# Turning the softmax results by VectorE's 32x32 transpose and a round trip through memory in place of TensorE's transposes

## The chip, the cores and the metric

One core of a Trainium2 chip runs the whole program. The metric is the device time of one execution in microseconds.

## What is computed

One layer of an encoder over two sequences of 512 tokens with 1024 channels, each with 256 memory tokens. After an RMS norm, one input projection gives the inputs of three branches (a state space model called S5, differential attention, cross-attention to the memory) and 3 x 1024 gates. The branches are projected up, gated and added, and an output projection and a feed-forward layer follow. The change concerns the two attentions. Cut to them:

```python
# cross-attention, 4 heads of 128, 256 memory tokens per sequence
s = jnp.einsum('blhd,bmhd->bhlm', q, mk).astype(jnp.float32) * (X_DH ** -0.5)
probs = jax.nn.softmax(s, axis=-1).astype(mv.dtype)
return jnp.einsum('bhlm,bmhd->blhd', probs, mv).reshape(Bn, L, X_WIDTH)

# differential attention, 4 heads with two maps of 64 each, 512 keys
s = jnp.einsum('bqhd,bkhd->bhqk', qblk, k).astype(jnp.float32) * scale
probs = jax.nn.softmax(s, axis=-1).reshape(Bn, DIFF_HEADS, 2, Q_BLOCK, L)
w = probs[:, :, 0] - lam * probs[:, :, 1]
return jnp.einsum('bhqk,bkhe->bqhe', w.astype(v.dtype), v)
```

## The kernel before

Every wide product is done in three passes of a rounded type: a value is split into a high part (a cast on ScalarE) and a low part (a subtraction on VectorE), and hi x hi, hi x lo and lo x hi are added in one PSUM bank. `split` issues that pair; `wf` is a weight as loaded (512 KB, two buffers), `wh` and `wl` are its parts.

The order of instructions on VectorE, ScalarE, GpSimd and SyncE is set by a scheduler. On TensorE it is the order of the program from the cross-attention on (`PE.on = True`). The kernel weaves two things there by hand: the steps of an attention, and *filler*, which is independent projection work. `units` is a generator for one 128-column tile of a projection: 48 products of 512 columns, handed out six at a time. `queue` is the list of such generators (queries of later heads, gates, values, then the branches' up projections, `merges`), and `fill(n)` issues about n of their products.

Cross-attention: 32 steps (4 heads, 2 sequences, 4 query tiles of 128). A step makes the scores of 128 queries against 256 memory tokens in a bank `sc`, and `softmax_parts` takes the maximum (`nb`, VectorE), the exponential `e` with its sum (ScalarE), and the reciprocal `r` (VectorE), after which VectorE scales `e`. The output product needs the keys on partitions, and so `e` is transposed: two transposes with `ident` on TensorE into a bank `tr` (`aux`), from where `split` takes them to `xpTh`, `xpTl`. After four steps the output product goes into a bank `oo`, and is stored to `bD`. Beside this, `Prepare` loads pieces of a later weight (`raw`), adds them on GpSimd, splits them (`hl`) and stores them (`wD`).

Differential attention: again 32 steps of 128 queries, now against 512 keys and with two maps. `score` makes both maps' exponentials and their weighted difference `e0`; `turn` transposes it with four TensorE transposes and splits it into `pH`, `pL`; `outputs` follows after every second step, `squares` and `normed` (the norm of a head's output, with transposes of their own in `tr`) after every fourth. The loop's lag is written out in its conditions, for example

```python
        if 0 < i <= n and steps[i - 1][2] % 2:
            outputs(i - 1)
```

In both stages the PSUM has eight banks: two `mm` (filler), three `sc`, two `tr`, one `oo`. All loads and stores of both stages are issued by SyncE, in one order.

Of the kernel before, what the change touches and what calls it, by code (L numbers as in the profile page):

```python
# [19 lines left out]
P = 128  # L20
L = 512
# [49 lines left out]
def encoder(ctx: ExitStack, tc: tile.TileContext, a, out, out_t):  # L71
# [68 lines left out]
    def split(hi, lo, src, scale=None):  # L140
# [6 lines left out]
            l_ = V.scalar_tensor_tensor(out=lo, in0=src, scalar=scale, in1=hi.bitcast(F32), op0=ALU.mult, op1=ALU.subtract)  # L147
        return h, l_

    last_w = last_s = None  # L150

    def weight_in(src, n=DM, parts=1, eng=SP):
# [138 lines left out]
    def mem_k(h, w):  # L291
        nonlocal mf
        o = aux()
        for i in range(KD):
            mm3([o], *w, [(mhk[i], mlk[i])], i, KD)
        if h % 2 == 0:
            mf = slot("ld", [P, 2, L], name="mf")
        S.copy(mf[:, h % 2], o)
        return mf

    ob = []
# [174 lines left out]
    for n in range(-(-(NC - 2) // STEPS)):  # L476
        wn = gate_w()
        next(s5)
        gate(*w)
        w = wn  # L480
        if n in (3, 4):
            ssm = sums(a["memN"], "ld", ss=None if n == 3 else ssm, ts=range(2 * n - 6, 2 * n - 4))
        if n == 5:
            rs_, bc = factor(ssm, DM)
            V.tensor_copy(mrs, rs_)
            S.copy(mbc, bc)
    for n in NG[1]:
        if n:
            wn = gate_w()
# [171 lines left out]
    queue = []  # L661
    owed = 0

    def fill(n):
        nonlocal owed
        owed += n
        while owed > 0 and queue:
            r = next(queue[0], None)
            if r is None:
                queue.pop(0)  # L670
            else:
                owed -= r
        if not queue:
            owed = 0
# [2 lines left out]
        while any(g is g_ for g_ in queue):  # L677
            fill(1)

    def units(src, hi, lo, use, nk=KD):  # L680

        wh, wl = weight(src, nk * P)
        for s in range(NS):
            cs = slice(s * L, (s + 1) * L)
            o = bank()
            for k in range(nk):
                mm3([o], wh, wl, [(hi[k][:, cs], lo[k][:, cs])], k, nk)
                if k == nk - 1:
                    use(s, o)
                if k % 2 == 1:  # L690
                    yield 6

    def gate_units():
        t = next(todo)
        gt = slot("ld", name="gt")

        def use(s, o):
            S.activation(out=gt[:, s * L : (s + 1) * L], in_=o, func=AF.Tanh, scale=0.5)

        yield from units(a["w_in"][20 + t], xh, xl, use)  # L700
        SP.dma_start(gD[t], gt)

    def v_units(hf, res):

        ws = [weight(a["w_v"][hf, c]) for c in range(2)]
        for s in range(NS):
            vh, vl = (slot("v2" if hf == 1 and s == 0 else "v", [P, 4, 256], F32R, n_) for n_ in ("vh", "vl"))
            for i2 in range(2):
                ob = bank()
                for kt in range(KD):  # L710
# [12 lines left out]
            res.append((vh, vl))  # L723
# [3 lines left out]
    def xq_units(h):  # L727
        def use(s, o):
            qs[h, s] = tuple(xa.tile([P, L], F32R, tag=n_, name=n_, bufs=3) for n_ in ("qh", "ql"))
            split(*qs[h, s], o)  # L730

        return units(a["w_in"][16 + h], xh, xl, use)

    ahead = [x_ for x_ in pieces if x_[2]]
    pes = ExitStack()
# [4 lines left out]
    for _ in xq_units(0):  # L740
        pass
    xq = {h: xq_units(h) for h in range(1, 4)}
    queue += [xq[1], gate_units(), xq[2], xq[3], v_units(0, v0), units(a["w_in"][4], xh, xl, dq0.__setitem__)]
    PE.on = True
    steps = [(h, s, lt) for h in range(4) for s in range(NS) for lt in range(4)]
    es, pT = {}, {}
    AHEAD = 2
    fill(6)
    for i in range(-AHEAD, len(steps) + 1):
# [19 lines left out]
        fill(4)  # L769
        if 0 <= i < len(steps):  # L770
            h, s, lt = steps[i]
            if lt == 0:
                pT[h, s] = tuple(slot("xT", [P, 2, L], F32R, n_) for n_ in ("xpTh", "xpTl"))
            e = es.pop(i)
            tr = aux()
            for j in range(2):
                PE.transpose(tr[:, j * P : (j + 1) * P], e[:, j * P : (j + 1) * P], ident)
            split(*(p_[:, :, lt * P : (lt + 1) * P] for p_ in pT[h, s]), tr[:, : 2 * P].rearrange("p (j q) -> p j q", j=2))
        fill(5 if i < len(steps) else 18)
        if i > 0 and steps[i - 1][2] == 3:  # L780
            h, s, _ = steps[i - 1]
            pTh, pTl = pT.pop((h, s))
            oo = bank("oo")
            hs = slice(h * P, (h + 1) * P)
# [24 lines left out]
    def rotated(is_q):  # L809
# [6 lines left out]
        def use(s, o):  # L816
# [8 lines left out]
            split(hl[:, 0], hl[:, 1], t1, scale=0.125 if is_q else None)  # L825
# [11 lines left out]
    qk = {}  # L837

    def qk_units(h, is_q):
        qk[h, is_q], use = rotated(is_q)  # L840
        yield from units(a["w_in"][(4 if is_q else 8) + h], xh, xl, use)


    mg = [None] * KD
# [10 lines left out]
        return list(zip(*(merge_part(n, t, tags[t]) for t in range(4))))  # L855

    def merge_units(n, b, m, first=False, last=False):
        gt = slot("ld", name="gl")
        SP.dma_start(gt, gD[n * KD + m])
        if first:  # L860
# [7 lines left out]
        yield from units(a["w_up"][n, m], *b, use, 4)  # L868
        if not first:
            PO.tensor_tensor(out=mg[m], in0=mg[m], in1=gt, op=ALU.add)  # L870
        if last:
# [10 lines left out]
            b0.append(list(zip(*(parts0[t_] for t_ in range(4)))))  # L882

    def merges():
        res_.close()
        xp_es.close()
        open_tags(mes, side="right", mg=8, y=8)
        for m in range(KD):
            if m == 5:
                b2 = merge_in(2)  # L890
            yield from merge_units(0, b0[0], m, first=True)
        for m in range(KD):
            yield from merge_units(2, b2, m)

    qk[0, True], use = rotated(True)
    for s in range(NS):
        use(s, dq0[s])
    for _ in qk_units(0, False):  # L900
        pass
    for _ in gate_units():
        pass
# [2 lines left out]
    queue += [qk_units(1, True), dk[1], gate_units(), qk_units(2, True), dk[2], v1_, qk_units(3, True), dk[3], gate_units(),  # L906
              gate_units(), merges()]
    s0, ss, osb = {}, {}, {}

    def score(i):  # L910
        nonlocal last_e
# [13 lines left out]
            er.append(softmax_parts(ap_, acol, sc[mp], L, 1.0, f"d{mp}", None if mp else s0[h, s][:, qt : qt + 1]))  # L925
        (e0, sm0), (e1, r1) = er
        V.scalar_tensor_tensor(out=r1, in0=r1, scalar=nlam, in1=sm0, op0=ALU.mult, op1=ALU.mult)
        last_e = last_x, V.scalar_tensor_tensor(out=e0, in0=e1, scalar=r1, in1=e0, op0=ALU.mult, op1=ALU.add)
        es[i] = e0

    def turn(i):
        h, s, qt = steps[i]
        if qt % 2 == 0:
            pT[h, s, qt // 2] = tuple(slot("pT", [P, 4, 2 * P], F32R, n_) for n_ in ("pH", "pL"))
        e0 = es.pop(i)
        tr = aux()
        for j in range(4):
            PE.transpose(tr[:, j * P : (j + 1) * P], e0[:, j * P : (j + 1) * P], ident)
        ps = slice(qt % 2 * P, qt % 2 * P + P)
        split(*(p_[:, :, ps] for p_ in pT[h, s, qt // 2]), tr.rearrange("p (j q) -> p j q", j=4))  # L940

    def outputs(i):

# [35 lines left out]
        SP.dma_start(bD[1, h, :, s * L : (s + 1) * L], osb[h, s])  # L979

    n = len(steps)
    for i in range(-1, n + 3):
        if i + 1 < n:
            score(i + 1)
        if i in (22, 23):
# [9 lines left out]
        if 1 < i <= n + 1 and steps[i - 2][2] == 3:  # L995
            squares(i - 2)
        if i > 2 and steps[i - 3][2] == 3:
            normed(i - 3)
    aes.close()
    phase.close()  # L1000
    ves.close()
# [16 lines left out]
        b1.append(merge_part(1, len(b1), "zzzy"[len(b1)]))  # L1018
    b1 = list(zip(*b1))
    for m in range(KD):  # L1020
        for _ in merge_units(1, b1, m, last=True):
            pass


# [1096 lines left out]
```

## Time and profile before

| | |
|---|---|
| median of 3 runs | 1583.21 us (1581.76 to 1584.73) |
| profiled execution: its time, its span | 1582.8 us, 1581.0 us |
| granted clock of TensorE | 0.999 |
| TensorE, VectorE, ScalarE, GpSimd busy | 1572.9, 1118.4, 628.3, 511.0 us |
| DMA | 261.06 MB, 165 GB/s over the span |

Busy time counts an instruction from its start to its end; matmuls overlap, so that what one of them costs is seen from start to start. A row of groups gives the line, engine, operation, out<-in, the count, the busy time, the mean duration of one, and the idle time before it with its releaser. Line 62 is a helper through which nearly all instructions are issued, so groups are read by the names of tiles. A DMA share is the mean busy share of the 16 DMA engines; the DMA view counts packets by size.

### The profile page before, as it was taken

What the parts mean: (1) busy time and instruction counts of PE and PEld (TensorE: products, weight loads), DVE (VectorE), ACT (ScalarE), POOL (GpSimd) and SP (SyncE); (2) the same over time, 40 slices, a digit from 0 to 9 for tenths busy, and PEclk for the clock granted to TensorE, in tenths of its full rate; (3) what the DMA queues carried; (4) which work ended last, traced back from release to release, by engine and by line L of the source; (5) the groups of instructions that cost most, each with busy time, mean ns of one, the idle gap of its engine ahead of it and who ended that gap; (6) DMA issues with size and microseconds to landing.
All of it is one profiled execution on the core that took longest, in us unless ns stands there. A gap on an engine that the chain in (4) does not pass through costs nothing.

```text
span 1581.0 us, 21523 instructions
## 1 busy us (share of the span) xinstructions
PE 1572.9 (99%) x7697; PEld 1321.3 (84%) x7697; DVE 1118.4 (71%) x1777; ACT 628.3 (40%) x1112; POOL 511.0 (32%) x406
## 2 busy tenths in 40 slices
PE   9999999999999999999999999999999999999998
PEld 8888888888898889888888888888888888788887
DVE  5797788565765776766445567777767777999664
ACT  7354333244543366564223353333333323333222
POOL 0001000001433221300343345767655542455352
PEclk9999999999999999999999999999999999999999
DMA  9543372556655543355544433555433241786632
GB/s 362 202 147 135 109 269 80 190 188 211 207 174 176 138 114 93 104 184 167 183 156 149 152 101 126 184 183 179 163 124 133 107 152 69 274 280 203 212 120 107
DMA packets 118971, 261.06 MB, mean 165 GB/s; under 512 B 15824, under 2 KB 51920, under 8 KB 118864
## 3 DMA queue, kind: packets, MB, share of 16 engines
q1 hardware_dynamic: 117424, 255.46, 48.6%
q10 hardware_dynamic: 1440, 4.22, 0.7%
q8 instruction: 61, 1.00, 0.3%
q14 instruction: 46, 0.38, 0.1%
HBM read 172.89 MB, written 74.15 MB: 156 GB/s over the span
## 4 chain that ended last, share of the span: by engine, by line
PE 94%; DMA 2%; DVE 2%; SPq 0%; issue 0%; ACT 0%; DVEq 0%; ACTq 0%
PE bkmm L62 82%; PE bktr L62 8%; PE bksc L62 3%; PE bkoo L62 2%; DMA zu<-uD 1%; SPq L62 0%; DMA yD<-y__2104 0%; DMA lv<-in_lamv 0%; DMA acc<-in_w_fo 0%; DMA zy<-yD 0%; DVE zu L62 0%; DVE y L62 0%; DMA wf<-in_w_mv 0%; DVE ts L62 0%; DVE zy L62 0%
## 5 line engine op out<-in xcount | busy, mean ns | idle before, releaser
L62 PE MATMUL bkmm<-xh,wh 128*128 128x512 f32 x640 | 252.7, 395 | 0.0
L62 PE MATMUL bkmm<-xl,wh 128*128 128x512 f32 x640 | 250.8, 392 | 0.0
L62 PE MATMUL bkmm<-xh,wl 128*128 128x512 f32 x640 | 250.0, 391 | 0.2 <-DVE wl L62 0.2
L62 PE MATMUL bkmm<-th,whl 128*128 128x512 f32 x696 | 227.2, 389 | 0.0
L62 ACT CAST wh<-wf 128x1024 fp32r<-128x1024 f32 (+1 forms) x131 | 116.1, 887 | 231.9 <-PE bkmm L62 199.5
L62 DVE TENSOR_TENSOR wl<-wf,wh 128x1024 fp32r<-128x1024 f32 (+1 forms) x132 | 140.6, 1065 | 65.4 <-ACT wh L62 62.4
L62 PEld LDWEIGHTS bkmm<-th,whl 128*128 128x128 f32 x696 | 130.6, 188 | 27.2 <-issue 0.2
L62 PEld LDWEIGHTS bkmm<-xh,wl 128*128 128x128 f32 x640 | 120.2, 188 | 26.1 <-DVE wl L62 0.7
L62 PE MATMUL bkmm<-th,w 128*128 128x512 f32 x432 | 140.4, 391 | 0.3
L62 PEld LDWEIGHTS bkmm<-xl,wh 128*128 128x128 f32 x640 | 120.4, 188 | 23.2 <-issue 0.6
L62 PEld LDWEIGHTS bkmm<-xh,wh 128*128 128x128 f32 x640 | 120.3, 188 | 23.2 <-issue 0.2
L62 POOL TENSOR_TENSOR raw<-raw 128x128 f32<-128x128 f32 x144 | 88.2, 613 | 156.7 <-DMA raw<-in_w_fo 107.1
L62 PE MATMUL bkmm<-tl,whl 128*128 128x512 f32 x348 | 135.4, 389 | 0.0
L62 POOL TENSOR_TENSOR ws<-wf 128x512 f32<-128x512 f32 x44 | 71.8, 1632 | 147.2 <-DMA wf<-in_w_fu 147.2
L62 DVE TENSOR_TENSOR whl<-ws,whl 128x1024 fp32r<-128x1024 f32 x44 | 77.2, 1755 | 57.5 <-ACT whl L62 57.5
L62 PE MATMUL bkmm<-th,wh 128*128 128x512 f32 x260 | 101.3, 390 | 0.0
L62 PE MATMUL bkmm<-th,wl 128*128 128x512 f32 x260 | 101.2, 389 | 0.0
L62 PE MATMUL bkmm<-tl,wh 128*128 128x512 f32 x260 | 101.2, 389 | 0.0
L62 PEld LDWEIGHTS bkmm<-th,w 128*128 128x128 f32 x432 | 80.9, 188 | 19.5 <-DVE nsq L62 1.1
L62 POOL TENSOR_TENSOR mg<-mg,gl 128x1024 f32<-128x1024 f32 x16 | 44.2, 2764 | 136.4 <-DMA bD<-osb 94.1
L62 PE MATMUL bkmm<-tl,w 128*128 128x512 f32 x216 | 84.1, 389 | 0.0
L62 ACT ACTIVATE e<-bksc,nb 128x512 f32<-128x512 f32 (+1 forms) x96 | 58.9, 616 | 60.8 <-DVE nb L62 60.1
(644 smaller groups left out, 3600.4 us busy)
## 6 DMA issues: line engine op xcount, KB each, us to landing
wf<-in_w_in SPq DMA_DIRECT2D x40, 512.0 KB, 4.4
wD<-hl SPq DMA_DIRECT2D x36, 512.0 KB, 2.9
w<-wD SPq DMA_DIRECT2D x36, 512.0 KB, 3.7
gD<-gt SPq DMA_DIRECT2D x24, 512.0 KB, 3.0
gl<-gD SPq DMA_DIRECT2D x24, 512.0 KB, 3.4
raw<-in_w_fo SPq DMA_DIRECT2D x88, 128.0 KB, 3.0
wf<-in_w_fg SPq DMA_DIRECT2D x22, 512.0 KB, 3.8
wf<-in_w_fu SPq DMA_DIRECT2D x22, 512.0 KB, 3.5
```

Source lines behind the costliest of these rows:

```text
L62: ins = do(*args, **kw)
```

## The change

No transpose of an attention's result is left on TensorE. In both attentions VectorE transposes the result `e` in blocks of 32x32 (`et`; in the differential attention into the buffer of the second map), SyncE stores it to memory (`xD`, `eD`), and `turned` loads it back with four loads, one for each 32 partitions, in which the blocks change places, into a tile `tn` of 128x1024 that is split as a whole. That is done once for four cross steps and once for two differential steps. So that a load reads runs of 32 columns times the number of key tiles (256 B with 256 memory tokens, 512 B with 512 keys), the keys' columns are permuted beforehand by `by_row` and `by_tile`, where the keys are written anyway. The scaling of `e` in the cross-attention moves from VectorE to ScalarE.

The output products move later: in the cross-attention from one step behind the block's last turning to six (the loop has 38 turns and `fill` gives 8 or 10 in each, 9 before), in the differential attention from one step to three, and `squares` and `normed` to four and six. A weight's load is now issued when its unit becomes the second in the queue, apart from the split (`yield 0` and `begun`). The value units take both banks of a sequence in turn, and the banks are three `mm`, three `sc`, one `tr`, one `oo`.

```diff
+    def turned(hl, src, nt):
+        nonlocal last_t
+        n = 32 * nt
+        t_ = slot("ld", [P, DM], name="tn")
+        tv = t_.rearrange("p (k f) -> p k f", f=n)
+        for d in range(4):
+            last_t = SP.dma_start(tv[32 * d : 32 * d + 32], src.rearrange("k (b x) f -> x (k b) f", b=4)[:, :, n * d : n * d + n])
+        split(*(p_.rearrange("p t (k q) -> p t k q", q=32) for p_ in hl), tv.rearrange("p k (t q) -> p t k q", q=32))
...
-    open_banks(mm=2, sc=3, tr=2, oo=1)
+    open_banks(mm=3, sc=3, tr=1, oo=1)
...
         while owed > 0 and queue:
+            for g in queue[:2]:
+                if not any(g is g_ for g_ in begun):
+                    begun.append(g)
+                    next(g)
...
-            last_e = last_x, V.tensor_scalar_mul(e, e, r)
-            es[i + AHEAD] = e
+            S.activation(out=e, in_=e, func=AF.Copy, scale=r)
+            et = xa.tile([P, NMEM], F32, tag="xt", name="et", bufs=4)
+            last_e = last_x, V.transpose(et, e)
+            SP.dma_start(xD[(i + AHEAD) // 4 % 2, lt], et)
...
-            if lt == 0:
+            if lt == 3:
                 pT[h, s] = tuple(slot("xT", [P, 2, L], F32R, n_) for n_ in ("xpTh", "xpTl"))
-            e = es.pop(i)
-            tr = aux()
-            for j in range(2):
-                PE.transpose(tr[:, j * P : (j + 1) * P], e[:, j * P : (j + 1) * P], ident)
-            split(*(p_[:, :, lt * P : (lt + 1) * P] for p_ in pT[h, s]), tr[:, : 2 * P].rearrange("p (j q) -> p j q", j=2))
-        fill(5 if i < len(steps) else 18)
-        if i > 0 and steps[i - 1][2] == 3:
+                turned(pT[h, s], xD[i // 4 % 2], 2)
+        fill(4 if i < 30 else 6)
+        if i >= 6 and steps[i - 6][2] == 3:
...
-        last_e = last_x, V.scalar_tensor_tensor(out=e0, in0=e1, scalar=r1, in1=e0, op0=ALU.mult, op1=ALU.add)
-        es[i] = e0
+        V.scalar_tensor_tensor(out=e0, in0=e1, scalar=r1, in1=e0, op0=ALU.mult, op1=ALU.add)
+        last_e = last_x, V.transpose(e1, e0)
+        SP.dma_start(eD[i // 2 % 4, i % 2], e1)
...
-        e0 = es.pop(i)
-        tr = aux()
-        for j in range(4):
-            PE.transpose(tr[:, j * P : (j + 1) * P], e0[:, j * P : (j + 1) * P], ident)
-        ps = slice(qt % 2 * P, qt % 2 * P + P)
-        split(*(p_[:, :, ps] for p_ in pT[h, s, qt // 2]), tr.rearrange("p (j q) -> p j q", j=4))
+            turned(pT[h, s, qt // 2], eD[i // 2 % 4], 4)
...
-        if 0 < i <= n and steps[i - 1][2] % 2:
-            outputs(i - 1)
+        if 3 <= i < n + 3 and steps[i - 3][2] % 2:
+            outputs(i - 3)
```

On TensorE, in the middle of the cross-attention, before (`bktr`, `bksc`, `bkoo`, `bkmm` are the banks, the products of `xh`, `xl` with `wh`, `wl` are filler):

```order
L62 MATMUL bkmm<-xh_132,wl 128x512
L62 MATMUL bktr<-ident,e 128x128 x2
L62 MATMUL bksc<-mkvh,qh 128x256
L62 MATMUL bksc<-mkvl,qh 128x256
L62 MATMUL bksc<-mkvh,ql 128x256
L62 MATMUL bkmm<-xh_133,wh 128x512
```

and now, where an output product stands right before a step's scores:

```order
L62 MATMUL bkmm<-xh_134,wl 128x512
L62 MATMUL bkoo<-xpTh,mkvh 128x512
L62 MATMUL bkoo<-xpTl,mkvh 128x512
L62 MATMUL bkoo<-xpTh,mkvl 128x512
L62 MATMUL bkoo<-xpTh,mkvh 128x512
L62 MATMUL bkoo<-xpTl,mkvh 128x512
L62 MATMUL bkoo<-xpTh,mkvl 128x512
L62 MATMUL bksc<-mkvh,qh 128x256
L62 MATMUL bksc<-mkvl,qh 128x256
L62 MATMUL bksc<-mkvh,ql 128x256
```

The pairs of transposes are gone from every step, and scores and output products alone are left between the filler.

On SyncE, in the same part of the program, before (`raw` and `wD` belong to `Prepare`):

```order
L62 DMA wD_2_3128<-hl 128x1024
L62 DMA raw<-in_w_fo 128x256
L62 DMA raw<-in_w_fo 128x2x128
L62 DMA gD<-gt 128x1024
L62 DMA wf<-in_w_v 128x1024
L62 DMA bD<-xosb 128x512
L62 DMA wD_0_3129<-hl 128x1024
```

and now:

```order
L62 DMA xD<-et 128x256 x2
L62 DMA wD_1_3132<-hl 128x1024
L62 DMA raw<-in_w_fo 128x256
L62 DMA raw<-in_w_fo 128x2x128
L62 DMA xD<-et 128x256 x2
L62 DMA wD_2_3133<-hl 128x1024
L62 DMA raw<-in_w_fo 128x256
L62 DMA tn<-xD 32x16x64 x4
L62 DMA raw<-in_w_fo 128x2x128
L62 DMA wf<-in_w_v 128x1024
```

Each block of four steps has put four stores and four loads between the transfers that stood there, and the loads wait for the stores.

More of the change, by code (lines that the diff above doesn't have):

```diff
@@ L297, in mem_k @@
             mf = slot("ld", [P, 2, L], name="mf")
-        S.copy(mf[:, h % 2], o)
+        for s in range(NS):
+            cs = slice(s * NMEM, (s + 1) * NMEM)
+            S.copy(by_row(mf[:, h % 2, cs], 2), by_tile(o[:, cs], 2))
         return mf
@@ L485, in encoder @@
             V.tensor_copy(mrs, rs_)
-            S.copy(mbc, bc)
+            for s in range(NS):
+                cs = slice(s * NMEM, (s + 1) * NMEM)
+                S.copy(by_row(mbc[:, cs], 2), by_tile(bc[:, cs], 2))
     for n in NG[1]:
@@ L824, in use @@
             hl = slot("ld", [P, 2, L], F32R, "hl")
-            split(hl[:, 0], hl[:, 1], t1, scale=0.125 if is_q else None)
+            if is_q:
+                split(hl[:, 0], hl[:, 1], t1, scale=0.125)
+            else:
+                split(*(by_row(hl[:, j], 4) for j in range(2)), by_tile(t1, 4))
             for mp in range(2):
@@ L839, in qk_units @@
     def qk_units(h, is_q):
+        u = units(a["w_in"][(4 if is_q else 8) + h], lambda s, o: use(s, o))
+        yield next(u)
         qk[h, is_q], use = rotated(is_q)
-        yield from units(a["w_in"][(4 if is_q else 8) + h], xh, xl, use)
+        yield from u
     mg = [None] * KD
@@ L857, in merge_units @@
     def merge_units(n, b, m, first=False, last=False):
+        u = units(a["w_up"][n, m], lambda s, o: use(s, o), 4, b)
+        yield next(u)
         gt = slot("ld", name="gl")
@@ L884, in merges @@
     def merges():
+        g = merge_units(0, lambda: b0[0], 0, first=True)
+        yield next(g)
         res_.close()
@@ L887, in merges @@
         open_tags(mes, side="right", mg=8, y=8)
[L888 to L893, printed above, removed]
+        b2 = []
+        for i in range(2 * KD):
+            if 2 <= i < 6:
+                b2.append(merge_part(2, i - 2, "y"))
+            if i + 1 < KD:
+                nxt = merge_units(0, lambda: b0[0], i + 1, first=True)
+            elif i + 1 < 2 * KD:
+                nxt = merge_units(2, lambda: list(zip(*b2)), i + 1 - KD)
+            if i + 1 < 2 * KD:
+                next(nxt)
+            yield from g
+            g = nxt
     qk[0, True], use = rotated(True)
@@ L899, in encoder @@
         use(s, dq0[s])
-    for _ in qk_units(0, False):
+    u = qk_units(0, False)
+    with tc.issue_after(last_t.ins):
+        next(u)
+    for _ in u:
         pass
@@ L981, in encoder @@
     n = len(steps)
-    for i in range(-1, n + 3):
+    for i in range(-1, n + 6):
         if i + 1 < n:
@@ L991, in encoder @@
             turn(i)
-        if 0 < i <= n and steps[i - 1][2] % 2:
-            outputs(i - 1)
+        if 3 <= i < n + 3 and steps[i - 3][2] % 2:
+            outputs(i - 3)
         fill(10)
[L995 to L998, printed above, removed]
+        if 4 <= i < n + 4 and steps[i - 4][2] == 3:
+            squares(i - 4)
+        if i >= 6 and steps[i - 6][2] == 3:
+            normed(i - 6)
     aes.close()
@@ L1020, in encoder @@
     for m in range(KD):
-        for _ in merge_units(1, b1, m, last=True):
+        for _ in merge_units(1, lambda: b1, m, last=True):
             pass
```

47 lines of the change are left out of this document (31 added, 16 removed).

## The prediction

> **What bounds the kernel now.** I read the page first, then TensorE's own waits, then the two attentions by windows, then single matmuls in the timeline, and last the groups of operations and the DMA view of the same windows. From the page (share of the span by engine, then the chain that ended last):
>
> ```profile
> span 1581.0 us, 21523 instructions
> PE 1572.9 (99%) x7697; PEld 1321.3 (84%) x7697; DVE 1118.4 (71%) x1777; ACT 628.3 (40%) x1112; POOL 511.0 (32%) x406
> PE 94%; DMA 2%; DVE 2%; SPq 0%; issue 0%; ACT 0%; DVEq 0%; ACTq 0%
> ```
>
> TensorE is busy for 99% of the span and carries 94% of the chain. Its waits on other engines (total us, times, longest) are four single ones over the whole span, and the longest is
>
> ```profile
> PE bkmm L62 <- DVE ident L62: 1.1, 1, 1.1
> ```
>
> So there is nothing on TensorE's side to be won but its own work. The windows are the cross-attention (first score to last output product), the differential attention, and one stretch that I need for the DMA engines:
>
> ```profile
> core 0: us, PE busy (x) PEld busy (x) DVE busy (x) ACT busy (x) POOL busy (x), PEclk, DMA share, GB/s
> 390.00:497.00 107.00, 107.00 (x638) 93.88 (x637) 72.92 (x202) 54.97 (x144) 38.50 (x66) 1.00 0.56 187
> 518.00:745.00 227.00, 227.00 (x1271) 195.90 (x1270) 166.06 (x311) 128.60 (x292) 37.09 (x24) 1.00 0.45 131
> 320.00:332.00 12.00, 12.00 (x54) 9.94 (x53) 7.10 (x22) 3.65 (x5) 0.00 (x0) 1.00 0.91 273
> ```
>
> In both attentions TensorE never stops, at full granted clock. What is taken off it is therefore saved, one for one, as long as what replaces it stays under cover; what replaces it lands on VectorE (68% and 73% busy) and on the DMA engines (0.56 and 0.45).
>
> **What is removed.** 192 transposes `bktr<-ident,e`, two in each of 32 cross steps and four in each of 32 differential steps:
>
> ```profile
> L62 PE MATMUL bktr<-ident,e x192: 270/272/276, 396.6 to 739.7; 128*128 128x128 f32 x192
> ```
>
> The bar of 272 ns is not the price, since matmuls overlap. The price is what a transpose adds between starts. One cross step and one differential step of TensorE's timeline (start, length):
>
> ```profile
> 484.47 0.39 PE L62 MATMUL bkmm<-xh,wl 128*128 128x512 f32 x1
> 484.71 0.38 PE L62 MATMUL bktr<-ident,e 128*128 128x128 f32 x2
> 484.84 0.48 PE L62 MATMUL bkmm<-xh,wh 128*128 128x512 f32 x1
> 485.16 0.39 PE L62 MATMUL bkmm<-xl,wh 128*128 128x512 f32 x1
> ...
> 621.71 0.28 PE L62 MATMUL bkmm<-wh,xl 128*128 128x256 f32 x1
> 621.83 0.60 PE L62 MATMUL bktr<-ident,e 128*128 128x128 f32 x4
> 622.18 0.36 PE L62 MATMUL bkoo<-pH,vh 128*128 128x256 f32 x1
> 622.38 0.28 PE L62 MATMUL bkoo<-pL,vh 128*128 128x256 f32 x1
> ```
>
> From 484.71 to 485.16 are 0.45 us for two transposes and a 512-wide product, which alone takes 0.23 (484.47 to 484.71 is 0.24): 0.22 us a step. From 621.83 to 622.38 are 0.55 us for four transposes and a 256-wide product of 0.12 (621.71 to 621.83): 0.43 us. 32 x 0.22 + 32 x 0.43 = 7.0 + 13.8 = **20.8 us**, all of it on the path. Since TensorE has no idle time here, this is also the most that the change can bring.
>
> **VectorE and ScalarE.** The groups of the two attentions (count | busy us, mean ns):
>
> ```profile
> L62 DVE TENSOR_REDUCE nb<-bksc 128x1 f32<-128x256 f32 x31 | 13.1, 421 | 10.3 <-PE bksc L62 9.6
> L62 DVE TENSOR_TENSOR xpTl<-bktr,xpTh 128x256 fp32r<-128x256 f32 x29 | 12.0, 413 | 0.1
> L62 DVE TENSOR_SCALAR e<-e,r 128x256 f32<-128x256 f32 x31 | 11.7, 376 | 0.7
> L62 DVE TENSOR_TENSOR wl<-wf,wh 128x1024 fp32r<-128x1024 f32 x7 | 9.0, 1281 | 6.1 <-ACT wh L62 6.1
> L62 ACT ACTIVATE e<-bksc,nb 128x256 f32<-128x256 f32 x31 | 14.8, 477 | 21.2 <-DVE nb L62 21.1
> L62 ACT CAST xpTh<-bktr 128x256 fp32r<-128x256 f32 x29 | 10.8, 373 | 6.4 <-PE bktr L62 6.2
> L62 ACT CAST wh<-wf 128x1024 fp32r<-128x1024 f32 x6 | 6.3, 1050 | 1.9 <-PE bkmm L62 1.9
> L62 DVE TENSOR_TENSOR pL<-bktr,pH 128x512 fp32r<-128x512 f32 x31 | 21.2, 683 | 1.5 <-ACT pH L62 1.3
> L62 DVE TENSOR_TENSOR wl<-wf,wh 128x1024 fp32r<-128x1024 f32 x10 | 14.2, 1422 | 0.0
> L62 DVE STREAM_SHUFFLE t<-bkmm 128x512 f32<-128x512 f32 x12 | 8.8, 736 | 0.0
> L62 ACT ACTIVATE acc<-bktr 128x128 f32<-128x128 f32 x28 | 7.4, 278 | 5.3 <-PE bktr L62 5.3
> ```
>
> No row shows the 32x32 transpose. Its nearest row is the shuffle, which also rearranges within 32 partitions: 736 ns for 512 columns. I take 0.74 us and 0.37 for 256 columns; the lower end is pL's 683, the upper twice the shuffle, 1.47, if filling and draining do not overlap. Cross: the scaling (32 x 0.376) goes to ScalarE, the subtractions from PSUM (32 x 0.413) become 8 on 1024 columns like wl (8 x 1.28): 72.9 - 12.0 - 13.2 + 11.8 + 10.2 = 69.7 us in the 100.0 that are left (107 - 7.0), 70%. Differential: 166.1 - 32 x 0.683 + 16 x 1.422 + 32 x 0.74 = 166.1 - 21.9 + 22.8 + 23.7 = 190.7 in 213.2 (227 - 13.8), 89%. I add **2 us** for this: the queue of VectorE is in order, and where a maximum comes late, the `sc` banks are held and the next scores wait; the ends are 0 and, at 1.47, the rival below. ScalarE stays about where it was: 32 scalings at some 0.37 come, and casts of 1024 columns at 1.05 take the place of four or two smaller ones.
>
> The Trainium skill (VectorE: DVE Perf Modes, The three transpose paths) has 311 ns for a 128x128 bf16 transpose on VectorE; by an estimate of four such, 1.24 us, the differential stage would hold 206.7 us of VectorE work, 97%, and the sum below would come to some 1586. No row here shows the operation.
>
> **The DMA engines.** New are 32 stores of 128 KB and 32 loads in runs of 256 B (cross), 32 stores of 256 KB and 64 loads in runs of 512 B (differential). The DMA view of the cross window, then of 80.5 to 85 us, where nearly all packets are 512 B, then of 48 to 49.2, where loads of 128 B a partition pass:
>
> ```profile
> DMA packets 10875, 20.06 MB, mean 187 GB/s; under 512 B 1008, under 2 KB 6384, under 8 KB 10864
> q1 hardware_dynamic: 10864, 19.93, 55.4%
> wf<-in_w_in SPq DMA_DIRECT2D x5, 512.0 KB, 3.7
> bD<-xosb SPq DMA_DIRECT2D x7, 256.0 KB, 2.4
> ...
> DMA packets 1083, 0.54 MB, mean 119 GB/s; under 512 B 122, under 2 KB 1073, under 8 KB 1081
> q1 hardware_dynamic: 1081, 0.52, 40.8%
> ...
> DMA packets 317, 0.21 MB, mean 178 GB/s; under 512 B 231, under 2 KB 231, under 8 KB 317
> q1 hardware_dynamic: 317, 0.21, 81.8%
> ```
>
> 512 B: 0.408 x 4.5 us x 16 engines = 29.4 us; over the 951 packets between 512 B and 2 KB (1073 - 122) that is 31 ns at most, call it 30. The stage's mean packet: 0.554 x 107 x 16 / 10864 = 87 ns. In the last row 0.818 x 1.2 x 16 = 15.7 us over 317 packets; if the 86 larger ones cost 87 each, the 231 small ones cost 36. So a 256 B packet lies between 15 (half of the 512 B one) and 36; I take **30**, since 128 B packets were no cheaper. The 1 KB packets of the stores lie between 30 and 87; I take 50.
>
> Cross: loads 32 x 512 x 30 ns / 16 = 30.7 us of all engines, stores 32 x 128 x 50 / 16 = 12.8, on top of 0.554 x 107 = 59.3: 102.8 us, in a stage that gives TensorE work for 100.0. Three weight and gate transfers (59.3 us / 19.93 MB x 0.5 = 1.5 us each) now stand behind the last load of turned results and need not be waited for: 98.3. The highest share that a stretch of this trace reaches is the 0.91 above: 98.3 / 0.91 = 108.0, that is **8 us** longer than TensorE's 100. By 15 ns it is 91 us and nothing is lost, by 36 ns 115 and 15 lost. The differential stage has room: 64 x 256 x 30 / 16 + 32 x 256 KB at 1.5 us per 0.5 MB = 30.7 + 24 on 0.444 x 227 = 101, 156 of 213.
>
> The Trainium skill (DMA: Bandwidth & Descriptors, Specifications) speaks against this change: a transfer under 512 B falls short of line rate, because the engine then reads, modifies and writes. By that rule the price could double, and the sum would be that of the second rival. By the row, small packets miss line rate but do not cost a multiple of a 512 B one.
>
> **The chain and the queues.** A block's path from its last score: maximum 0.42, exponential 0.48, scaling 0.37, transpose 0.37, store 2.4 (bD<-xosb), four issues and at most the 3.7 of a weight to land, cast 1.05, subtraction 1.28: with the small operations between some 13 us. Issues cost SP 11.49 / 24 = 0.48 us each:
>
> ```profile
> 191.08 11.49 SPq L1953 DMA_DIRECT2D w<-gD  x24
> ```
>
> Before the output product stand eight turns of eight filler products and a score: 8 x (8 x 0.23 + 3 x 0.12) = 18 us. So some 5 us are to spare, until DMA falls behind. The new waits: SP waits for the four stores before the first load of a block, and for VectorE before each store; behind it stand raw, wD and the next wf. ScalarE's cast waits for four loads; behind it stand the next exponentials, and behind these the `sc` banks and TensorE. SP gets 160 more issues, 77 us in the 313 of both stages; I cost them at nothing, since SP computes nothing, and if it has no room for them, they delay the loads as slower packets would.
>
> Costed at nothing: the earlier weight loads (3.7 us to land against a unit of 48 products, 11 us; uncovered, 6 us once), v's new order, the third `mm` bank, and one `tr` bank instead of two (squares and factors lie two turns, some 14 us at 227 / 32 each, apart; uncovered, four transposes and four squares of 0.28, some 2 us, eight times). The loop runs three turns longer, and 132 products of the queue (912, less 39 turns of 20), 30 us, remain behind it to cover the last head's way out through memory; uncovered, some 8 us once.
>
> **Sum.** The profiled execution took 1582.8, the median shown is 1583.2, so both stand for the same. 1582.8 - 20.8 + 8 + 2 = **1572.0 us**. What a measurement of this kernel can tell from no change is 0.2%, 3.2 us.
>
> **The rivals.** *All hidden:* 256 B packets cost under 23 ns (then 91 us of DMA at 0.91 fit into 100), or the loads catch up in the last blocks, which have no raw and wD beside them; then 1582.8 - 20.8 = 1562. For it: DMA idles at 44% before, and the spare 5 us. Against it: 98 us of DMA in 100.
>
> *Small runs sink the cross stage (slower):* a 256 B packet costs twice the 512 B row, 60 ns. Then loads take 61.4, the stage 129.0 / 0.91 = 142, 42 lost: 1582.8 - 20.8 + 42 + 2 = 1606. It decides from where the loss reaches 18.8: 118.8 x 0.91 - 67.6 = 40.5 us of loads, 40 ns a packet. For it: my price stands only a quarter below that. Against it: the 36 ns of the row with 128 B loads.
>
> *VectorE sets the differential stage (slower):* at 1.47 us a transpose it has 214 us of work in 213, and if it can fill 90% of its time, as it must wait for ScalarE in each step, the stage takes 238: 25 lost, 1582.8 - 20.8 + 8 + 25 = 1595. It decides at 12.8 lost, 1.14 us a transpose. For it: 89% at my own price. Against it: the shuffle's 736 ns.
>
> That transposes stay is excluded: the order of the changed kernel has none of `e`.
>
> **Chances.** The forecast (4 to 17 us lost in all, 1566 to 1579) 0.42; all hidden 0.24; small runs 0.19; VectorE 0.15. Faster are the first two, 0.66; the two others split into 0.06 for the same (their near ends, 1580 to 1586) and 0.28 for slower. The range reaches from 1561 (all hidden, a microsecond below) to 1590: 36 ns give 1579, and half of the way to VectorE's upper end, 11 more, 1590. What is left out is the far end of the two slow cases, some 0.19.
>
> **What will show it.** Right: no `bktr<-ident,e`, no PE gap but some microseconds before `bkoo<-xpTh` from the fourth block on, released by ScalarE or VectorE behind a tn load, and a DMA share near 0.9 in the cross stage. Wrong: a share below 0.8 there, with no wait (packets cheaper); waits of over 20 us before `bkoo`, or before `bksc` in the differential stage; a transpose row over 1.1 us.

## The result and the profile after

The changed kernel took 1588.3 us (median; 1583.46 to 1592.46 in 20 runs) against 1582.77 (1581.13 to 1586.48 in 20 runs) for the kernel before: ratio 1.003, interval 1.0022 to 1.0039. It is **slower by 5.5 us**, where 1572.0 was forecast; 1588.3 lies inside the range, at its upper end. Its profiled execution took 1584.59 us, so the trace has 1.8 of the 5.5 us to explain.

From the page of the changed kernel: span, engines, and the chain that ended last.

```profile
span 1582.8 us, 21354 instructions
...
PE 1559.1 (99%) x7505; PEld 1307.1 (83%) x7505; DVE 1146.6 (72%) x1769; ACT 636.8 (40%) x1109; POOL 514.6 (33%) x406
...
PE 79%; DMA 7%; DVE 6%; ACT 2%; issue 2%; SPq 2%; POOL 1%; DVEq 0%; ACTq 0%; POOLq 0%
```

The 192 transposes are gone (7697 products before, 7505 now), but TensorE's busy time fell by 13.8 us and not by 20.8, and TensorE has lost 15 points of the chain, most of them to DMA, VectorE and ScalarE. What TensorE waits for (us in total, times, longest), where 1.1 was the longest before:

```profile
PE bksc L62 <- ACT e L62: 10.0, 4, 3.7
PE bkmm L62 <- DVE mg L62: 2.1, 1, 2.1
PE bkoo L62 <- DVE xpTl L62: 2.0, 2, 1.5
```

The same windows as before (busy times of TensorE, weight loads, VectorE, ScalarE, GpSimd; granted clock, DMA share, GB/s), with the densest stretch of the cross stage between them:

```profile
390.00:497.00 107.00, 104.90 (x593) 91.37 (x592) 75.43 (x182) 68.19 (x154) 41.49 (x66) 1.00 0.86 271
420.00:450.00 30.00, 30.00 (x200) 27.60 (x199) 22.15 (x61) 21.28 (x51) 14.15 (x24) 1.00 0.97 290
518.00:745.00 227.00, 216.57 (x1123) 184.55 (x1122) 182.31 (x318) 121.71 (x269) 37.08 (x24) 0.97 0.64 190
```

The cross stage holds: DMA runs at 0.97 for 30 us, and TensorE loses 2 us. The differential stage does not: 10.4 us idle, and the granted clock is 0.97 instead of 1.00. The groups there (count | busy, mean ns | idle before, releaser):

```profile
L62 DVE STREAM_TRANSPOSE e<-e 128x512 f32<-128x512 f32 x32 | 22.6, 705 | 0.3
...
L62 DVE TENSOR_TENSOR pL<-tn,pH 128x1024 fp32r<-128x1024 f32 x15 | 18.4, 1227 | 12.1 <-ACT pH L62 12.1
...
L62 ACT CAST pH<-tn 128x1024 fp32r<-128x1024 f32 x15 | 15.7, 1046 | 29.8 <-DMA tn<-eD 29.8
```

The durations are what the prediction took (0.70 us a transpose, 1.05 a cast, 1.23 a subtraction). New are the last columns: ScalarE stands 29.8 us at the head of its queue waiting for loads, and VectorE 12.1 us behind ScalarE. Before, the same two waits were

```profile
ACT pH L62 <- PE bktr L62: 7.5, 11, 1.4
...
DVE pL L62 <- ACT pH L62: 2.5, 5, 1.1
```

How TensorE comes to stop is seen at the longest gap, in the timelines of ScalarE, VectorE and TensorE of the changed kernel (start, length, [idle before]):

```profile
579.61 1.05 ACT L62 CAST pH<-tn 128x1024 fp32r<-128x1024 f32 x1 [2.20 <-DMA tn<-eD]
583.21 0.63 ACT L62 ACTIVATE hl<-t 128x512 fp32r<-128x512 f32 x1 [2.55 <-POOL t L62]
583.86 1.28 ACT L62 ACT_TABLE_LOAD   x1
585.15 0.69 ACT L62 ACTIVATE e<-bksc,nb 128x512 f32<-128x512 f32 x1
```

```profile
579.72 0.71 DVE L62 STREAM_TRANSPOSE e<-e 128x512 f32<-128x512 f32 x1
580.69 1.36 DVE L62 TENSOR_TENSOR pL<-tn,pH 128x1024 fp32r<-128x1024 f32 x1 [0.27 <-ACT pH L62]
581.97 1.28 DVE L62 TENSOR_REDUCE nb<-bksc 128x1 f32<-128x512 f32 x2
```

```profile
576.95 0.39 PE L62 MATMUL bksc<-l,q 128*128 128x512 f32 x1
...
581.93 0.40 PE L62 MATMUL bksc<-l,q 128*128 128x512 f32 x1
585.98 0.50 PE L62 MATMUL bksc<-h,q 128*128 128x512 f32 x1 [3.66 <-ACT e L62]
586.32 0.55 PE L62 MATMUL bksc<-l,q 128*128 128x512 f32 x1
...
587.09 0.63 PE L62 MATMUL bkmm<-xl,wh 128*128 128x512 f32 x1
587.52 0.63 PE L62 MATMUL bkmm<-xh,wl 128*128 128x512 f32 x1
...
590.20 0.40 PE L62 MATMUL bkmm<-xh,wh 128*128 128x512 f32 x1
590.43 0.39 PE L62 MATMUL bkmm<-xl,wh 128*128 128x512 f32 x1
```

The scores of a step were complete by 577.3, but their maxima (`nb`) were made only at 581.97, behind `pL`. The loads have little part in that: VectorE had other work until 580.43 and stood idle for 0.27 us. The exponential then stood behind `hl` (the split of the rope's result), which waited 2.55 us for GpSimd's `t`, and behind a table load of 1.28 us. Two of the three `sc` banks were held for nine microseconds, and TensorE, needing the second bank of the next step, stopped for 3.66 us. In the gap of 3.30 us no cast of turned results stands between 651.47 and 673.49; the exponential stood behind `hl` and a table load alone (lines of the three engines' timelines, others left out):

```profile
669.60 1.24 DVE L62 TENSOR_REDUCE nb<-bksc 128x1 f32<-128x512 f32 x2
670.22 0.62 ACT L62 CAST hl<-t 128x512 fp32r<-128x512 f32 x1 [4.67 <-POOL t L62]
670.86 1.28 ACT L62 ACT_TABLE_LOAD   x1
672.15 0.69 ACT L62 ACTIVATE e<-bksc,nb 128x512 f32<-128x512 f32 x1
672.98 0.80 PE L62 MATMUL bksc<-h,q 128*128 128x512 f32 x1 [3.30 <-ACT e L62]
```

The loads alone are seen at the other two gaps, of 1.13 us (568.80) and 1.92 us. At the second the maxima were done by 610.62, and the cast stood before the exponential, 5.03 us in wait of its loads (again with others left out):

```profile
609.35 1.27 DVE L62 TENSOR_REDUCE nb<-bksc 128x1 f32<-128x512 f32 x2
612.51 1.05 ACT L62 CAST pH<-tn 128x1024 fp32r<-128x1024 f32 x1 [5.03 <-DMA tn<-eD]
613.57 1.28 ACT L62 ACT_TABLE_LOAD   x1
614.87 0.69 ACT L62 ACTIVATE e<-bksc,nb 128x512 f32<-128x512 f32 x1
615.70 0.50 PE L62 MATMUL bksc<-h,q 128*128 128x512 f32 x1 [1.92 <-ACT e L62]
```

So of the 10.0 us before `bksc` 3.05 stand behind waits for loads, and 6.96 end behind `hl`. ScalarE's wait for GpSimd's `t` is not new: 17.5 us in this stage before, when TensorE never stopped, and 12.7 now. Why it stops TensorE now, and how much of that the loads and VectorE's added work have brought about, this trace does not show; the experiments below bear on it.

A gap costs twice. After it, 512-wide products start 0.43 us apart until 589.65 and 0.23 us apart again from 590.20: half rate for some 3.4 us. The windows of 8 us behind this gap and behind those of 3.30 (at 673) and 2.05 us (at 754) read

```profile
586.00:594.00 8.00, 8.00 (x34) 6.66 (x35) 6.32 (x10) 2.90 (x7) 2.56 (x2) 0.79 0.55 172
...
673.00:681.00 8.00, 8.00 (x29) 6.68 (x30) 6.28 (x13) 3.96 (x9) 0.00 (x0) 0.65 0.89 240
754.00:762.00 8.00, 7.90 (x40) 6.80 (x41) 4.46 (x8) 1.21 (x2) 0.00 (x0) 1.00 0.93 305
```

With the gap of 1.92 us at 615.7 (0.79 too) that is 8 x (0.21 + 0.21 + 0.35) = 6.2 us of clock. Together: -20.8 for the transposes, +2.0 before `bkoo`, +10.0 before `bksc`, +2.1 before the up projection, +1.5 in small waits (2.2 now, 0.7 before), +6.2 clock: +1.0, where the two profiled executions differ by 1.8. The median run lies 3.7 us above the profiled one. The mean clocks of the 20 runs are 0.993 to 0.996 (before's profiled run: 0.999), and the profiled run's 0.995 is the middle one, so the clock does not account for the 3.7 us; no trace here does.

### The profile page after: what moved, and what is told of

Read it like the earlier page. It is cut to its first block, busy times and chain, and to the rows that moved or that the text cites. A ratio compares the mean times of both kernels' runs of the same rounds, so it can differ in the third digit from the quotient of the medians.

```text
span 1582.8 us, 21354 instructions
## 1 busy us (share of the span) xinstructions
PE 1559.1 (99%) x7505; PEld 1307.1 (83%) x7505; DVE 1146.6 (72%) x1769; ACT 636.8 (40%) x1109; POOL 514.6 (33%) x406
## 4 chain that ended last, share of the span: by engine, by line
PE 79%; DMA 7%; DVE 6%; ACT 2%; issue 2%; SPq 2%; POOL 1%; DVEq 0%; ACTq 0%; POOLq 0%
PE bkmm L62 71%; PE bktr L62 6%; SPq L62 2%; DMA tn<-eD 1%; DVE e L62 1%; PE bkoo L62 1%; PE bksc L62 1%; ACT e L62 1%; DVE t L62 1%; DMA eD<-e 1%; POOL t L62 1%; DVE nb L62 1%; DMA tk<-in_xN 1%; DMA c_n<-cD 1%; DMA zu<-uD 1%
## 5 line engine op out<-in xcount | busy, mean ns | idle before, releaser
L62 POOL TENSOR_TENSOR raw<-raw 128x128 f32<-128x128 f32 x144 | 93.6, 651 | 143.5 <-DMA raw<-in_w_fo 107.8
L62 POOL TENSOR_TENSOR ws<-wf 128x512 f32<-128x512 f32 x44 | 68.5, 1556 | 146.4 <-DMA wf<-in_w_fu 137.8
```

Of the source, the lines that this page charges most:

```text
L62: ins = do(*args, **kw)
```

## The experiments

**Theory 1**: the loss is in the order. A split that waits for its four loads stands in the queues of ScalarE and VectorE ahead of later exponentials and maxima, these hold the `sc` banks, and TensorE stops. **Theory 2**: the small runs of the loads are too dear. **Theory 3**: VectorE has too much work in the differential stage. Ratios are to the kernel before, with their intervals.

**One turn later.** The split of a differential pair is kept behind the exponentials and the transpose of the next turn; nothing else changes.

```diff
-            turned(pT[h, s, qt // 2], eD[i // 2 % 4], 4)
+            late.append(((h, s, qt // 2), turned_in(eD[i // 2 % 4], 4)))   # the four loads, as before
...
+        turn_late()   # behind score(i + 1): with tc.issue_after(last_e[0].ins), tc.issue_after(last_e[1].ins): the split
```

> Theory 1 (order of ScalarE's queue): the cast of the turned results waits for its loads, the next exponentials stand behind it, the score banks are held and TensorE stops and loses clock. With the split of the differential attention issued one turn later, behind that turn's exponentials and transposes, the four gaps before bksc (10 us) and the lower clock behind them (some 7 us) go: 1566 to 1572 us. Theory 2 (DMA: the small runs and the volume make the loads late) and theory 3 (VectorE at 80% cannot keep up): within 4 us of the changed kernel's 1588.

1580.02 us, 0.9973 (0.9963 to 0.9983): 8.3 us better than the changed kernel, where nothing was moved by hand but one cast and one subtraction (the scheduler orders the rest anew around them), and faster than before. 1566 to 1572 were expected. The waits of TensorE, and in the stage (518 to 745 us) those of ScalarE:

```profile
PE bksc L62 <- ACT e L62: 6.1, 4, 2.0
...
ACT pH L62 <- DMA tn<-eD: 10.9, 7, 4.0
```

The wait for loads fell to a third, not to nothing, and only a part of what was expected came: one turn is still too short for store, issue and landing. The long gap keeps its shape, with `hl` and a table load before the exponential, and falls from 3.66 to 2.05 us; the one of 3.30 us is gone.

**One plain load instead of four** (runs of 1 and 2 KB). This kernel leaves out the exchange of the quadrants.

```diff
-        for d in range(4):
-            last_t = SP.dma_start(tv[32 * d : 32 * d + 32], src.rearrange("k (b x) f -> x (k b) f", b=4)[:, :, n * d : n * d + n])
+        last_t = SP.dma_start(t_.rearrange("p (k f) -> p k f", f=P * nt), src.rearrange("k p f -> p k f"))
```

> One load of the same bytes in rows of 4 KB in place of the four loads with exchanged quadrants, in both attentions (the exchange of quadrants is left out). Theory 2: the DMA share of the cross stage falls from 0.86 to below 0.7 and all of the loss goes, 1563 to 1567 us. Theory 1: the loads land some us earlier (one issue instead of four with other transfers between), so part of the gaps goes, 1572 to 1583 us. Theory 3: 1588.

1581.51 us, 0.999 (0.9982 to 0.9999): 6.8 us better than the changed kernel, but far from the 1563 to 1567 that theory 2 had. Large runs and a quarter of the issues take 1.7 of the 2.0 us before `bkoo` in the cross stage away and shorten the gaps; in all `bksc` still waits 10.0 us, in 7 waits of at most 2.7. ScalarE's wait for loads in the differential stage is no shorter (34.2 us, 29.8 in the changed kernel), so this sum alone does not measure the loss. Most of the 6.8 us are in no trace: the two profiled executions differ by 0.3 us. The DMA view of that stage, changed kernel first, then this one:

```profile
q1 hardware_dynamic: 32576, 28.84, 85.9%
```

```profile
q1 hardware_dynamic: 19693, 28.31, 79.3%
```

The 16384 packets of 256 B that were 4096 of 1 KB cost (0.859 - 0.793) x 107 x 16 = 113 us of engine time more. With 30 to 87 ns for a 1 KB packet, the bounds of the prediction, a 256 B packet is estimated at 14 to 29 ns, below the 30 that was taken. Theory 2 and the number of issues together are worth some 2 us in the cross stage and at most 5 in the differential one.

**Each attention alone.** First the cross-attention, with the differential attention as before and the banks shared out anew between the stages.

> Only the cross-attention is turned by VectorE and memory; the differential attention has TensorE's transposes, its old lags and its old banks. Theory 1: 7.0 us gained, some 2 lost before the first output product: 1577 to 1579 us, clock 1.00. Theory 2 in its strong form (the cross stage is where 256 B runs cost): 1583 or more.

1589.35 us, 1.0036 (1.0024 to 1.0048). This says nothing of the change: the sharing out itself stopped TensorE, as the first row of its waits shows.

```profile
PE bkmm L62 <- DVE t L62: 6.9, 1, 6.9
PE bkoo L62 <- DVE xpTl L62: 1.9, 2, 1.5
```

So it was built again, with the new sharing out behind the first gate unit, where a third `mm` bank is no longer needed:

```diff
     for _ in gate_units():
         pass
+    open_banks(mm=2, tr=2, sc=3, oo=1)
```

> The change in the cross-attention alone; the differential attention as before, and the banks are shared out anew only behind the first gate unit, so that a third bank is there while the rope reads the queries. Theory 1 (the loss lies in the differential stage, where the split waits for its loads ahead of the next maxima and exponentials): the 64 transposes save 7.0 us, TensorE waits 2 to 3 us before bkoo, 1576 to 1579. Rival (the DMA engines pace the cross stage at some 8 us, or the new order costs on its own): 1583 or more.

1581.04 us, 0.9993 (0.9984 to 1.0001). TensorE waits 2.2 us before `bkoo` and never for an exponential. The 2 us to the kernel before cannot be told from nothing; 4 to 7 were expected. The trace, of one of the longer runs (1584.35 us), has the reason: over the span TensorE's waits add up to 7.9 us in eleven single ones, none over 1.5, against 1.8 before, and take 6.1 of the 7.0 us back. Then the differential attention alone, with the cross-attention as before:

> Only the differential attention is turned by VectorE and memory; the cross-attention has TensorE's transposes, its old lag and its old banks. Theory 1: the whole loss stays, and 7.0 us of gain are missing, 2 of loss too: 1589 to 1595 us with a clock below 1.00 between 560 and 700 us. Theory 2 in its strong form: 1569 to 1573 us.

1601.89 us, 1.0108 (1.0091 to 1.0126). 1589 to 1595 were expected. The waits before `bksc` are there without a changed cross stage, and larger:

```profile
PE bksc L62 <- ACT e L62: 12.2, 7, 4.1
PE bkmm L62 <- DVE t L62: 3.3, 1, 3.3
```

Its size is again spoiled by the banks (the 3.3) and by waits of 1.5 and 1.8 us that the two `mm` banks bring to the cross stage. That waits before `bksc` come with the differential stage alone is clear even so.

**Two turns later.** Load as in the change, split behind the exponentials of the second next turn, products one turn later (the norm too).

```diff
+        if late and late[0][0] < i - 1:   # the pair of two turns ago: issue_after(last_e), then the split
...
-        if 3 <= i < n + 3 and steps[i - 3][2] % 2:
-            outputs(i - 3)
+        if 4 <= i < n + 4 and steps[i - 4][2] % 2:
+            outputs(i - 4)
```

> The loads of a pair are issued in the turn of the change, its split into pH and pL not before the second next turn's maxima and exponentials, its output products one turn later. Theory 1: ScalarE's wait for tn falls from 35 us to under 8, VectorE's wait for pH under 5, TensorE's wait before bksc under 4 in all, 1566 to 1573. Rival (VectorE's and ScalarE's own work, not the loads, makes the maxima late): waits before bksc stay at 6 to 10, 1578 to 1583.

1574.64 us, 0.9949 (0.9937 to 0.9962): just above what theory 1 had (1566 to 1573). The same waits, and VectorE's:

```profile
PE bksc L62 <- ACT e L62: 4.3, 5, 2.2
...
ACT pH L62 <- DMA tn<-eD: 7.4, 2, 5.8
...
DVE pL L62 <- ACT pH L62: 2.7, 1, 2.7
```

ScalarE's wait for loads went 29.8, 10.9, 7.4 us with each turn, TensorE's before `bksc` 10.0, 6.1, 4.3, and the time 1588.3, 1580.0, 1574.6. ScalarE's wait for GpSimd's `t` stays, at 13.7 us in this stage; so that wait alone does not stop TensorE for long.

**The loads a turn later too.**

```diff
-            late.append((i, (h, s, qt // 2), turned_in(eD[i // 2 % 4], 4)))
+            pairs.append((i, (h, s, qt // 2)))   # loads behind the next turn's last_e
```

> As the kernel with the split two turns later, but the four loads too are issued a turn later, so that SP finds the two stores landed and tn holds its buffer a turn less. Theory 1: as that kernel, 1566 to 1573, or a little better if the buffers of hl, gt and yt (the same four) are short there; 2 to 4 us worse than that kernel if the landing of the loads is what is still short. Rival: 1578 to 1583 like one turn.

1579.52 us, 0.9979 (0.997 to 0.9988). 4.9 us worse than with the loads at their old place. SyncE now waits less for the stores to land (9.5 us in the stage, 15.6 before this edit), and ScalarE longer for the loads (14.2, 7.4 before). So what is short is the time for landing; neither SyncE's waiting for stores nor the four buffers that `tn` shares can be what cost more, as both were eased.

**No memory in the differential attention.** The split reads VectorE's transposed tile where it lies, and the output products come a turn earlier than in the change. This kernel leaves out the exchange of the quadrants.

```diff
-        SP.dma_start(eD[i // 2 % 4, i % 2], e1)
+        es[i] = e1
...
-            turned(pT[h, s, qt // 2], eD[i // 2 % 4], 4)
+        split(*(p_[:, :, ps] for p_ in pT[h, s, qt // 2]), es.pop(i).rearrange("p (j q) -> p j q", j=4))
```

> In the differential attention the store and the loads are left out: the split reads VectorE's transposed tile where it lies (the exchange of quadrants is left out), once for each step, and the output products come one turn earlier. VectorE keeps its 32 transposes and has 32 subtractions of 512 instead of 16 of 1024, some 3 us more. Theory 1 (the waits for the loads): no wait of ScalarE for tn, waits before bksc under 3 us, 1563 to 1569. Rival (VectorE's load): waits before bksc stay at 8 to 12 us and the clock falls as in the changed kernel, 1578 to 1588.

1568.92 us, 0.9912 (0.9898 to 0.9925). Of the 20.8 us 14 appear once nothing in the differential stage waits for a load of turned results, although VectorE is as busy there (third figure behind the stage's length) as with the split two turns later (189.0 us):

```profile
518.00:745.00 227.00, 224.05 (x1194) 191.94 (x1194) 188.69 (x346) 129.20 (x298) 36.64 (x24) 1.00 0.47 138
```

The later output products of the two kernels before this one are not what helps, since here they come earlier. This edit takes the stores, the loads and their issues away together; that the order alone is worth 13.7 us, the kernel with the split two turns later shows. Of TensorE's waits are left

```profile
PE bksc L62 <- ACT e L62: 2.9, 3, 1.3
PE bkoo L62 <- DVE xpTl L62: 1.8, 2, 1.3
```

**Every transpose twice**, on the kernel with the split two turns later.

```diff
+        V.transpose(e1, e0)
         last_e = last_x, V.transpose(e1, e0)
```

> The kernel with the split two turns later (1574.6), with every 32x32 transpose of the differential attention done twice: 32 x 0.71 = 22.7 us more on VectorE, nothing else moved. Theory 1 (what counts is what a wait in the queue holds back; VectorE at 80% has room): VectorE rises to some 90% of the stage, waits before bksc grow by a few us, 1575 to 1581. Rival (VectorE's share sets the stage, as the third rival of the prediction had it, from 90% on): 15 us or more are lost, 1590 or more.

1582.02 us, 0.9993 (0.9984 to 1.0001): 7.4 us more than without. The differential stage by windows with one transpose a step:

```profile
518.00:745.00 227.00, 222.64 (x1166) 189.23 (x1165) 189.04 (x329) 123.97 (x275) 38.56 (x24) 0.99 0.70 208
```

and with two:

```profile
518.00:745.00 227.00, 214.92 (x1118) 181.61 (x1117) 200.14 (x350) 120.95 (x268) 34.84 (x24) 0.98 0.66 198
```

32 x 0.705 = 22.6 us of work cost 7.4 us of time: a third of it is paid. That is a microsecond more than theory 1 had, and 8 less than theory 3: at 83% of the stage (189.0 of 227) VectorE's work is not free, but it does not set the stage either. By this price the work that the change itself adds to VectorE (188.7 - 166.1 = 22.6 us in the kernel without memory) would cost some 7 us, an estimate, and 6.7 are what that kernel lacks of the 20.8.

**What is left.** The cross-attention's products a turn later, and then the split of the rope's result kept behind its turn's exponentials.

```diff
-        if i >= 6 and steps[i - 6][2] == 3:
+        if i >= 7 and steps[i - 7][2] == 3:
```

> As the kernel with the split two turns later, and in the cross-attention the output products one turn later too (seven turns behind the last step of a block instead of six). Theory 1: the 2.6 us before bkoo in the cross stage go, 1571 to 1574. Rival (the loads are DMA-paced there, and a turn more only moves the wait): no change, 1574 to 1577.

1573.84 us, 0.9947 (0.9935 to 0.9959). The wait before `bkoo` falls from 2.6 to 0.4 us; the 0.8 us of the median cannot be told from nothing. It is the fastest version that keeps the whole computation: 8.5 us below the kernel before, measured beside it, and 14.5 below the changed one.

```diff
+            with tc.issue_after(last_e[0].ins), tc.issue_after(last_e[1].ins):
                 split(...)   # hl
```

> As the kernel with the later cross outputs, and the split of the rope's result (hl, which waits for GpSimd's t on ScalarE) is not queued before the exponentials and the transpose of its turn. If the waits of ScalarE for GpSimd's t are what still holds the maxima and exponentials: waits before bksc fall from 4.3 to under 2, 1568 to 1572. If the keys and queries then come too late instead: waits for l<-hl or q<-hl of 2 us or more, 1573 to 1580.

1575.66 us, 0.9959 (0.9946 to 0.9971): nothing gained, and ScalarE's wait for GpSimd's `t` is as long as before (20.4 us against 19.9 from 497 to 770). The scheduler had found that order itself. `hl` still stands ahead of the next turn's exponentials in both (3.78 us of waiting before the ones at 658.45 and 660.46), so the run does not say what that wait costs. What the remaining 4 to 5 us before `bksc` hang on stays open; the kernel without memory has 2.9 of them too, so at most some 2 are the loads.

## Why the prediction was wrong

- *What bounds the kernel, and the 20.8 us.* Right: TensorE's busy time fell by 13.8 us, and the lower clock, at which its products take longer, hides 6.2 more. The kernel without memory in the differential stage fits it too: 1582.8 - 20.8 + 1.8 + 2.9 = 1566.7 by its waits, 1568.9 measured.
- *Durations.* Right: 0.705 us a transpose for 0.74, and no rival that needed 1.14 or more. By an estimate from a figure of the Trainium skill (VectorE: DVE Perf Modes, The three transpose paths: 311 ns for 128x128 bf16) it would have been 1.24. The rows of 705 ns for 128x512 decide against that sum.
- *The DMA term, +8.* Mis-sized: 2.0 us before `bkoo`. The price of a 256 B packet was at or above the upper end (14 to 29 ns, taken 30), and 0.91 was no ceiling: the stage ran at 0.97 for 30 us. The kernel before had shown as much, and the prediction misread its trace in calling 0.91 the highest share. From 12 to 44 us the share there is 1.00 or more in every stretch of 12 us, with TensorE busy throughout; the first of them:

```profile
12.00:24.00 12.00, 12.00 (x53) 9.82 (x52) 5.30 (x7) 9.46 (x14) 0.00 (x0) 1.00 1.00 392
```

Divided by 1.00, the prediction's own 98.3 us of DMA fit into TensorE's 100, and the term would have been nothing. The slow rival fell too: the small packets cost 113 of the stage's 1471 us of engine time (0.859 x 107 x 16). The Trainium skill (DMA: Bandwidth & Descriptors, Specifications) has transfers under 512 B fall short of line rate by a read-modify-write. No doubled price shows here: an estimated 14 to 29 ns for a packet of 256 B stand beside at most 31 for the 512 B packets of the prediction's row; per byte, with 31 taken, that is 0.9 to 1.9 times as much, which leaves the line rate open.
- *VectorE in the differential stage, +2.* This is the step that failed. It went from a share (89% busy) to a small wait. The share was no worse than that, and what cost time was a wait *inside* the queue. The prediction named it in "The chain and the queues": "ScalarE's cast waits for four loads; behind it stand the next exponentials, and behind these the `sc` banks and TensorE", and gave it no price. It also did the sum of the block's path, 13 us against 18, only for the cross stage; and it had no word of VectorE's own wait, `pL` behind `pH`, with the next maxima behind. Measured: 10.0 us before `bksc`, of which the loads alone stand before 3.05; before the other 6.96 stands `hl` with its wait for GpSimd, likewise in ScalarE's queue and likewise without a price. Moving the split back, to the second next turn, brought the median from 1588.3 to 1574.6, gaps and clock together. So most of the time went with waits at the head of these queues; how the loads turned the old wait of `hl` into gaps is not shown.
- *The clock.* Every gap was priced at its length. 6.2 us more were paid in half-rate products behind three of them. That and the gaps make up the profiled run to within 0.8 us; the 3.7 us by which the median lies above it stay open.
- *SyncE's issues at nothing.* Not told apart: one load in place of four saves issues and small packets together, and both together are worth at most 6.8 us. SyncE waited 18.0 us in the differential stage for stores of turned results to land.
- *The signs to look for.* "Over 20 us before `bkoo` or `bksc`" was too high a bar: 10.0 us sufficed, with the clock behind it. The waits before `bkoo` came at the first and the fourth block, not from the fourth on.

## What to carry to other kernels

Where an engine that runs in order waits for a load, price what stands behind it in that queue, not the share of time in which it is busy; then place the waiting instruction behind the work of as many turns as the load needs to land (here two, worth 13.7 us), before counting the way through memory as free. A TensorE that never stops should be read as one whose gaps cost their length and, from about 1.5 to 2 us on, often the clock behind them.

## What the runs showed of the hardware

The granted clock fell after gaps of 1.44 us and more, though not after all of them. In the traces of the changed kernel and the eleven experiments, from 380 to 800 us, 12 of 13 gaps of 2.19 us or more were followed by half-rate products (0.79 or less over the next 8 us), 7 of 18 between 1.44 and 2.06 us, and none of 23 between 0.88 and 1.37 us (one more, of 1.09, is left out, as a gap of 3.12 us followed it within the 8 us). The same wait before `bkoo` at 418 to 420 us dropped the clock in two kernels (1.44 and 1.48 us, 2 us behind another gap of 0.80 and 0.44) and left it at 1.00 in three (1.48, 1.49 and 1.51, the second behind another of 0.65). The Trainium skill (TensorE: Matmul & The Clock Gate, Why this matters for your kernels) warns of idle gaps of over some 3 us between bursts. The half-rate stretch of 3.4 us agrees with the free-running window of 3.4 us that it gives (What's actually happening); the length of the gap does not, as gaps of half to two thirds of that cost the clock.

The Trainium skill (TensorE: Matmul & The Clock Gate, Architectural detail) has ScalarE and VectorE work strictly in order. The timelines agree: VectorE stood idle for 0.27 us before `pL` at 580.69 and made the maxima behind it, at 581.97, though their scores were there at 577.3.

Sixteen DMA engines were kept at 0.97 for 30 us by loads of 256 B runs, stores and weights together, 290 GB/s, and TensorE was busy for all of them.
